# The gates' 16 columns of w_in ride with the first head's v group, which moves to second place, and the scans get a third stream

## The chip, the core and the metric

The kernel runs on one core of one Trainium2 chip. The metric is the device time of one execution in microseconds (us); the kernel before takes 2905.36 us, the median of three runs (2904.51 to 2906.1). A core has five engines that run side by side and wait for each other through semaphores: TensorE (PE in the profile, with its weight loads as PEld), VectorE (DVE), ScalarE (ACT), GpSimd (POOL) and SyncE (SP). Each takes its instructions in the order in which they were built. Transfers between the main memory and the core's own memory are issued from the queues of SP, POOL and ACT; TensorE's results land in eight PSUM banks, of which four are named mm and four sd here.

## The reference, cut to what matters

```python
hn = rmsnorm(x, norm1_w[l])
proj = hn @ w_in[l]                      # 512 x 2048 times 2048 x 11280
conv_out = centred_depthwise_conv(proj[..., :SHORT_CONV_CH], conv_w[l], conv_b[l])
rest = proj[..., SHORT_CONV_CH:]
...                                      # four hyena blocks: long convolutions of conv_out
qk = jax.nn.silu(conv_out[..., 3 * HW:])
v = rest[..., :MW].reshape(B, L, H, dh)
o = jax.nn.sigmoid(rest[..., MW:2 * MW])
g = rest[..., 2 * MW:2 * MW + N_MLSTM_GATES].reshape(B, L, 4, H) + mlstm_gate_bias[l]
h_fwd = mlstm_direction(q, k, v, g[:, :, 0], g[:, :, 1])
h_bwd = flip(mlstm_direction(flip(q), flip(k), flip(v), flip(g[:, :, 2]), flip(g[:, :, 3])))
y_b = o * (h_fwd + h_bwd)
mixed = gate_a * (y_a @ w_branch_a[l]) + gate_b * (y_b @ w_branch_b[l])
x = x + mixed @ w_out[l]
x = x + (jax.nn.silu(gu[..., :FFN_HIDDEN]) * gu[..., FFN_HIDDEN:]) @ w_down[l]   # gu = rmsnorm(x) @ w_gate_up
return rmsnorm(x, norm_f_w)
```

One matrix, w_in, feeds everything: the hyena channels, q, k, v and o of four heads, 16 gate columns, and the two merge gates. The gates g are an input and a forget value of every token, head and direction, 16 numbers a token.

## The kernel before, in words

A product is made in three matmuls (mm3, L72), since every operand is split into a high and a low part: high x high, high x low, low x high. The weights are split by ScalarE (a cast, L170) and VectorE (a subtraction, L171), in units of 256 rows by 256 columns.

The first stage works through the columns of w_in in groups of 256. `group_feat` (L198) holds the weights still and moves 512 tokens, so one of its matmuls has 512 columns; `group_v` (L229) holds the tokens still and moves 256 columns of weights, because v is wanted with the tokens on the partitions. `group_v` needs four PSUM banks of the mm pool, `group_feat` two. The order of the groups is a list written out by hand (`groups`, L1134): the first hyena block, the second, head 0, the third and fourth hyena blocks, heads 1 to 3, the four o groups. `Weights` (L174) makes the split weights two units ahead of their use, in just that order. `w_in_cols` (L1139) yields once after every unit.

`gate_cols` (L431) makes the 16 gate columns behind the first group: it loads 16 columns at a time (rows of 64 bytes), puts their high and low parts side by side into an otherwise zero 128 x 128 tile, and multiplies that with 512 tokens, 32 matmuls in all. The result has the gates on the partitions; four small matmuls with a selection matrix (`sel32`) turn it round, add high and low, and give `gates` with tokens on the partitions.

Beside the groups run the side streams: `stream_b` makes the hyena filters and their spectra and later some sums of x for the merge (`combos_x`), `stream_a` the gate rows (`gate_rows`, L459: logarithms, running sums and running maxima of the gates), then the hyena convolutions and the scan of the heads (`mlstm`, L839), in the order hyena 0 and 1, head 0, hyena 2 and 3, heads 1, 2, 3. `turns` (L971) takes from the streams by turns; every piece states its cost. `drive` (L254) goes through the groups, and gives the side streams 2.6 units of cost per step (RATIO, L1130), saved up to two steps. A stream whose input isn't ready yields "wait". What is left of the streams when the groups are done is run off by a loop behind `drive`. After that a scheduler, which belongs to the framework, orders each engine's instructions by readiness; nothing can pass an instruction that its tile depends on.

A scan of one head loads q and k, splits them, makes four score tiles S (24 matmuls of 512 columns), loads v, and then runs eight units, four in each direction: exponential (ScalarE, L896), mask (GpSimd, L899), product with S (VectorE, L901), split (ScalarE L904, VectorE L905), 3 to 12 matmuls of 258 columns, denominator and result (L927 to L934). Then 8 transposes (L940), two copies (L942) and two stores into d_yb (L943). Its tiles come from the pool pr.

The second stage is the merge: 16 groups of w_in by the class `Winograd`, seven products of 24 matmuls each (L70 with 256 columns), with weights loaded in four quarters (wr and r, L1056). The quarters wr have a pool of their own, the quarters r lie in memory that belonged to pr: their loads wait until the tiles that lay there are done with. Then follow the two branches, w_out, the gate and up matrices and the down matrix, which the change does not touch.

Of the kernel before, what the change touches and what calls it, by code (L numbers as in the profile page):

```python
# [8 lines left out]
F32 = mybir.dt.float32  # L9
# [25 lines left out]
def hybrid_block_kernel(ctx, tc, x, norm1_w, w_in, conv_w, conv_b, filt_w1, filt_b1, filt_freq1,  # L35
# [27 lines left out]
    def mm_ps():  # L63
        return new(pm, "mm")

    def sd_ps():
        return new(psd, "sd")
# [14 lines left out]
        return h, l  # L82


    csm = new(cp, "csm", (P, 3 * P + 16))
# [4 lines left out]
    sel32 = csm[0:32, 3 * P:3 * P + 16]  # L90
    onesf = new(cp, "onesf", (P, P))
    nc.vector.memset(onesf, 1.0)

# [63 lines left out]
        return bc  # L157


    def load_a(w, r0, c0, nk=4, ncol=256):  # L160
        n_tile[0] += 1
        raw = wpool[0].tile([P, nk, ncol], F32, tag="wr", name=f"wr_{n_tile[0]}", bufs=3)
        nc.sync.dma_start(raw, w[r0:r0 + nk * P, c0:c0 + ncol].rearrange("(k p) c -> p k c", p=P))
        return raw

    def split_w(src, shape):
# [7 lines left out]
    class Weights:  # L174
# [6 lines left out]
        def get(self, c0, kb):  # L181
            assert self.units[self.given] == (c0, kb)
            while len(self.made) < min(self.given + 1 + self.ahead, len(self.units)):
                uc, uk = self.units[len(self.made)]
                if uk % 4 == 0:
                    self.raw = load_a(w_in, uk * P, uc)
                self.made.append(split_w(self.raw[:, uk % 4:uk % 4 + 2, :], [P, 2, 256]))
            self.given += 1
            return self.made[self.given - 1]

# [37 lines left out]

    def group_v(w, c0, act, ahead=None):  # L229

        ps = [mm_ps() for _ in range(4)]
        units = w_units(w, 0, KB, c0)
        first = None
        for u in range(0, KB, 2):
            h, l = next(units) if ahead is None else ahead.get(c0, u)
            if u == 0:
                first = (h, l)

            for tb, v, (wh, wl) in ([(tb, u, (h, l)) for tb in (0, 1)] + ([(2, 0, first), (3, 0, first)] if u == 2 else [])
                                    + ([(2, u, (h, l)), (3, u, (h, l))] if u else [])):  # L240
                ts = slice(tb * P, (tb + 1) * P)
                for k in range(2):
                    kb = v + k
                    aH, aL = act[kb]
                    mm3(ps[tb][:, 0:256], aH[:, ts], aL[:, ts], wh[:, k, :], wl[:, k, :],
                        kb == 0, kb == KB - 1)
            yield None
        yield ps
# [177 lines left out]
    a_col = new(cp, "a_col", (P, 2, 4, 4))  # L426
    em_col = new(cp, "em_col", (P, 2, 4, 4))

    gates_t = []

    def gate_cols():  # L431
        gps = mm_ps()
        for u in range(0, KB, 4):
            raw = load_a(w_in, u * P, C_G, 4, 16)
            n_tile[0] += 1
            g = wp.tile([P, 4, P], F32R, tag="wh", name=f"wg_{n_tile[0]}", bufs=4)
            nc.vector.memset(g.bitcast(F32), 0.0)
            nc.vector.tensor_copy(g[:, :, 0:16], raw)
            nc.vector.tensor_tensor(g[:, :, 16:32], raw, g[:, :, 0:16].bitcast(F32), ALU.subtract)
            for k in range(4):  # L440
                kb = u + k
# [3 lines left out]
        gb = new(cp, "gb", (32, 1))  # L445
        nc.vector.memset(gb, 0.0)
        nc.gpsimd.dma_start(gb[0:16], mlstm_gate_bias[0].rearrange("g h -> (g h)").rearrange("(n o) -> n o", o=1))
        gT = gt()
        nc.vector.tensor_tensor(gT[0:32], gps[0:32], rbc[0:32], ALU.mult)
        nc.vector.tensor_scalar(gT[0:32], gT[0:32], gb, None, ALU.add)  # L450
        ps = sd_ps()
        for tb in range(4):
            mm(ps[:, tb * 16:(tb + 1) * 16], gT[0:32, tb * P:(tb + 1) * P], sel32, True, True)
        gates = new(cp, "gates", (P, 4, 2, 2, 4))
        gates_t.append(gates)
        nc.vector.tensor_copy(gates.rearrange("p a b c d -> p (a b c d)"), ps[:, 0:64])
        done.add("gates matmul")

    def gate_rows():  # L459
        yield from need("gates matmul")  # L460
        gates = gates_t[0]

        n = [0]

        def sm(shape=(P, 32)):
            n[0] += 1
            return pr.tile(list(shape), F32, tag=f"gs{n[0]}", name=f"gs{n[0]}", bufs=1)
# [79 lines left out]
    def filter_net():  # L547
        tables = []
        for m in range(4):
            t = gt()  # L550
            nc.sync.dma_start(t, c_dft[m])
            tables.append(t)
        vec = new(ph, "fvec", (P, 4))
        for j, src in enumerate((filt_b1, filt_freq1, filt_b2, filt_freq2)):
            for half in range(2):
                nc.sync.dma_start(vec[half * 64:half * 64 + 64, j:j + 1], src[0].rearrange("(n o) -> n o", o=1))
        w1 = new(ph, "fw1", (33, 2, 64))
        w2 = new(ph, "fw2", (64, 2, 64))
# [5 lines left out]
        nc.sync.dma_start(csm[:, P:3 * P + 16], c_small[:, P:3 * P + 16])  # L564
# [24 lines left out]
        ps = sd_ps()  # L589
        mm(ps, w2.rearrange("p a b -> p (a b)"), h1[0:64], True, True)  # L590
        yield 4
        hh = sin_layer(ps, vec[:, 2:3], vec[:, 3:4])
        h2["H"] = new(ph, "h2H", dt=F32R)
        h2["L"] = new(ph, "h2L", dt=F32R)
        nc.scalar.copy(h2["H"], hh)
        nc.vector.tensor_tensor(h2["L"], hh, h2["H"].bitcast(F32), ALU.subtract)
        yield 4
# [530 lines left out]
    N_PLAIN = 4  # L1128
    AHEAD = 2
    RATIO = 2.6  # L1130
    side = turns(stream_b(), stream_a())

    parts = (("hy", 1), ("hd", 0), ("hy", 2), ("hy", 3), ("hd", 1), ("hd", 2), ("hd", 3))
    groups = [HW, 2 * HW]  # L1134
    for kind, n in parts:
        groups += [b + 256 * n for b in ((0, HW, 2 * HW) if kind == "hy" else (C_Q, C_K, C_V))]
# [405 lines left out]
```

## Time and profile before

| what | value |
|---|---|
| median of three runs | 2905.36 us (2904.51 to 2906.1) |
| the profiled execution's own time | 2905.68 us |
| its span, first to last instruction | 2903.9 us |
| TensorE busy | 2869.5 us (99%) |
| VectorE busy | 2106.6 us (73%) |
| ScalarE busy | 1274.0 us (44%) |
| granted TensorE clock, mean | 0.996 |
| w_in groups end, merge begins | about 834 us |

In a timeline's row stand the start, the duration, the engine, the line, the operation, what it writes and reads, the shape, and how many equal ones follow each other; in brackets the idle time of that engine before it and what ended it. A matmul's duration reaches until its result has landed, and the next starts earlier: the rate is read from the distance between starts. "L70" is the helper mm, so nearly all matmuls have that line, and they are told apart by tiles: mm<-a,wh is a group of w_in, mm<-wh,a a v group, sd<-g,g a scan.

### The profile page before, as it was taken

The page shows a single profiled execution, that of the slowest core. Times are in us where ns is not written, and L with a number is a line of the kernel's source. Part 1 is how long each engine was busy: PE and PEld are TensorE (multiplying, and loading weights), DVE is VectorE, ACT ScalarE, POOL GpSimd, SP SyncE. Part 2 cuts the span into 40 slices and gives each one's busy share as a digit, 9 for nine tenths or more (in the row PEclk, how much of TensorE's full clock was granted, in tenths as well). Part 3 has the DMA queues.
Part 4 walks back from the last instruction along what each step waited for, and adds up shares of the span by engine and source line. Part 5 has one row for each costly group of instructions (what it writes and reads, how often), then busy time and mean ns, then how long its engine had stood idle before and what let it go on. Part 6 is the DMA issues. An engine that isn't in the chain of part 4 may idle for free.

```text
span 2903.9 us, 48189 instructions
## 1 busy us (share of the span) xinstructions
PE 2869.5 (99%) x18412; PEld 2595.7 (89%) x18412; DVE 2106.6 (73%) x3844; ACT 1274.0 (44%) x2267; POOL 186.2 (6%) x431
## 2 busy tenths in 40 slices
PE   9999999999999999999999999999999999999998
PEld 7888887898889999888899999999999998888886
DVE  7897977889478888454549888888888885233336
ACT  5434354436565555222435444444444444233224
POOL 0101011102210001000110000000000000000000
PEclk9999999999999999999999999999999999999999
DMA  5334334334444444743434333333433327343433
GB/s 179 120 109 131 116 120 135 110 115 139 149 126 129 131 140 138 246 138 94 151 122 130 124 118 117 121 119 117 126 123 113 120 89 227 100 124 119 127 109 131
DMA packets 285589, 377.01 MB, mean 130 GB/s; under 512 B 18620, under 2 KB 222852, under 8 KB 285357
## 3 DMA queue, kind: packets, MB, share of 16 engines
q1 hardware_dynamic: 261339, 298.36, 33.2%
q0 software_dynamic: 22752, 73.44, 7.5%
q8 instruction: 144, 2.36, 0.3%
q10 hardware_dynamic: 1266, 2.13, 0.2%
q14 instruction: 88, 0.72, 0.1%
HBM read 326.67 MB, written 47.20 MB: 129 GB/s over the span
## 4 chain that ended last, share of the span: by engine, by line
PE 93%; DVE 3%; DMA 2%; issue 2%; ACT 1%; POOL 0%; SPq 0%; DVEq 0%; POOLq 0%; ACTq 0%
PE mm L70 66%; PE sd L70 26%; DMA wr<-in_w_down_dram 1%; DVE wl L171 0%; DVE st L374 0%; PE sd L289 0%; PE sd L725 0%; PE sd L1301 0%; DMA bt<-d_o 0%; DVE st L371 0%; DVE h L81 0%; DMA xt<-in_x_dram 0%; DMA g<-d_q 0%; DMA g<-d_hy 0%; DVE T L1329 0%
## 5 line engine op out<-in xcount | busy, mean ns | idle before, releaser
L171 DVE TENSOR_TENSOR wl<-wr,wh 128x512 fp32r<-128x512 f32 x512 | 350.6, 688 | 485.9 <-ACT wh L170 480.9
L170 ACT CAST wh<-wr 128x512 fp32r<-128x512 f32 x512 | 316.4, 621 | 763.5 <-PE mm L70 707.7
L70 PE MATMUL mm<-a,wh 128*128 128x512 f32 (+1 forms) x2136 | 626.9, 376 | 0.0
L70 PE MATMUL mm<-T,h 128*128 128x256 f32 x2592 | 463.8, 282 | 3.9 <-ACT h L1047 3.9
L70 PE MATMUL sd<-T,h 128*128 128x256 f32 x2592 | 461.5, 281 | 0.0
L70 PEld LDWEIGHTS mm<-a,wh 128*128 128x128 f32 x2136 | 387.7, 190 | 69.4 <-issue 4.1
L70 PE MATMUL mm<-a,wl 128*128 128x512 f32 (+1 forms) x1068 | 400.8, 375 | 1.9 <-DVE wl L171 1.4
L70 PEld LDWEIGHTS mm<-T,h 128*128 128x128 f32 x2592 | 398.5, 189 | 4.4 <-ACT h L1047 4.4
L70 PE MATMUL mm<-wh,h 128*128 128x512 f32 x1280 | 395.8, 391 | 3.6 <-ACT h L80 3.6
L70 PEld LDWEIGHTS sd<-T,h 128*128 128x128 f32 x2592 | 397.2, 189 | 0.0
L1047 ACT CAST h<-s 128x512 fp32r<-128x512 f32 x395 | 245.0, 621 | 276.6 <-PE sd L70 134.3
L70 PE MATMUL mm<-T,l 128*128 128x256 f32 x1296 | 363.5, 281 | 0.8 <-DVE l L1048 0.8
L70 PE MATMUL sd<-T,l 128*128 128x256 f32 x1296 | 362.7, 280 | 0.0
L70 PEld LDWEIGHTS mm<-wh,h 128*128 128x128 f32 x1280 | 241.4, 189 | 54.0 <-ACT h L80 3.8
L1048 DVE TENSOR_TENSOR l<-s,h 128x512 fp32r<-128x512 f32 x395 | 270.2, 685 | 12.0 <-ACT h L1047 9.6
L1047 ACT CAST h<-r 128x512 fp32r<-128x512 f32 x285 | 177.0, 621 | 215.0 <-PE mm L70 105.3
L70 PE MATMUL mm<-wh,a 128*128 128x256 f32 (+1 forms) x1152 | 259.8, 319 | 0.0
L70 PE MATMUL mm<-wl,h 128*128 128x512 f32 x640 | 249.7, 391 | 0.0
L70 PEld LDWEIGHTS mm<-T,l 128*128 128x128 f32 x1296 | 246.2, 190 | 1.2 <-DVE l L1048 1.2
L70 PEld LDWEIGHTS sd<-T,l 128*128 128x128 f32 x1296 | 245.6, 189 | 0.0
L70 PEld LDWEIGHTS mm<-a,wl 128*128 128x128 f32 x1068 | 202.5, 190 | 37.9 <-DVE wl L171 2.9
L1048 DVE TENSOR_TENSOR l<-r,h 128x512 fp32r<-128x512 f32 x285 | 191.5, 686 | 45.7 <-ACT h L1047 45.5
(365 smaller groups left out, 4358.3 us busy)
## 6 DMA issues: line engine op xcount, KB each, us to landing
r<-in_w_gate_up_dram SPq DMA_DIRECT2D x176, 512.0 KB, 4.7
wr<-in_w_in_dram SPq DMA_DIRECT2D x144, 512.0 KB, 3.8
wr<-in_w_down_dram SPq DMA_DIRECT2D x88, 512.0 KB, 3.6
r<-in_w_in_dram SPq DMA_DIRECT2D x32, 512.0 KB, 4.8
wr<-in_w_out_dram SPq DMA_DIRECT2D x32, 512.0 KB, 4.8
d_h<-xo POOLq DMA_DIRECT2D x44, 256.0 KB, 2.6
hl<-d_h SPq DMA_DIRECT2D x44, 256.0 KB, 3.5
d_g<-xo POOLq DMA_DIRECT2D x32, 256.0 KB, 4.3
```

The source lines that it names most:

```text
L70: nc.tensor.matmul(o, a, b, start=start, stop=stop)
L170: nc.scalar.copy(h, src)
L171: nc.vector.tensor_tensor(l, src, h.bitcast(F32), ALU.subtract)
L1047: nc.scalar.copy(h, a)
L1048: nc.vector.tensor_tensor(l, a, h.bitcast(F32), ALU.subtract)
```

## The change

The gate columns lose their own matmuls. The loads of the first head's v columns bring the 16 gate columns with them, in a second transfer for each load, the split runs over 272 columns, and `group_v` moves 272 columns where it moved 256. The result has the tokens on the partitions at once: four VectorE instructions scale it and add the bias. The first head's v group now stands second in the list of groups, where `gate_cols` stood, and no longer behind q and k of head 0. `gate_rows` becomes a third stream beside the two, and takes its small tiles from one g tile.

```diff
-    def load_a(w, r0, c0, nk=4, ncol=256):
+    def load_a(w, r0, c0, nk=4, ncol=256, extra=False):
...
+        if extra:
+            nc.sync.dma_start(raw[:, :, ncol:n], w[r0:r0 + nk * P, C_G:C_G + 16].rearrange("(k p) c -> p k c", p=P))
...
-                    self.raw = load_a(w_in, uk * P, uc)
-                self.made.append(split_w(self.raw[:, uk % 4:uk % 4 + 2, :], [P, 2, 256]))
+                    self.raw = load_a(w_in, uk * P, uc, extra=uc == C_V)
+                self.made.append(split_w(self.raw[:, uk % 4:uk % 4 + 2, :], [P, 2, 272 if uc == C_V else 256]))
...
-                    mm3(ps[tb][:, 0:256], aH[:, ts], aL[:, ts], wh[:, k, :], wl[:, k, :],
+                    mm3(ps[tb][:, 0:n], aH[:, ts], aL[:, ts], wh[:, k, :], wl[:, k, :],
...
+        if h:
+            yield from v_cols(h)
+
+    def v_cols(h):
         for r in group_v(w_in, C_V + h * 256, X, ahead):
...
+            if h == 0:
+                nc.vector.scalar_tensor_tensor(gates[:, tb].rearrange("p b c d -> p (b c d)"), r[tb][:, 256:272],
+                                               rstd[:, tb:tb + 1], gbias, ALU.mult, ALU.add)
         done.add(("v", h))
+        if h == 0:
+            done.add("gates matmul")
...
-    def gate_cols():
-        gps = mm_ps()
-        for u in range(0, KB, 4):
-            raw = load_a(w_in, u * P, C_G, 4, 16)
...
-                mm(gps, g[:, k, :], X[kb][0], kb == 0, False)
-                mm(gps, g[:, k, :], X[kb][1], False, kb == KB - 1)
-            yield
...
-            mm(ps[:, tb * 16:(tb + 1) * 16], gT[0:32, tb * P:(tb + 1) * P], sel32, True, True)
...
     def stream_a():
-        yield from gate_rows()
         yield from need("filter")
...
-    side = turns(stream_b(), stream_a())
+    side = turns(stream_b(), stream_a(), gate_rows())
...
-    groups = [HW, 2 * HW]
+    groups = [C_V, HW, 2 * HW]
...
-        yield from hyena_cols(0, gate_cols())
+        yield from hyena_cols(0, v_cols(0))
```

In the changed program lines stand some 11 lower in number from `gate_rows` on (L940 is L929, L1056 is L1044).

The first place is TensorE's order behind the first group. mm_233 is that group's second bank, rb are the tiles that spread the norm over a row; before, wg are the gates' weights:

```order
L70 MATMUL mm_233<-a_460,wl_465 128x512
L111 MATMUL sd_481<-csm_72,rows_a_79 128x120
L70 MATMUL sd_538<-csm_72,rb_539 128x128
L70 MATMUL mm_570<-a_214,wg_573 128x512
L70 MATMUL mm_570<-a_215,wg_573 128x512
L70 MATMUL mm_570<-a_218,wg_573 128x512
L70 MATMUL sd_538<-csm_72,rb_542 128x128
L70 MATMUL mm_570<-a_219,wg_573 128x512
```

And now, with wh and wl the first v unit:

```order
L70 MATMUL mm_233<-a_460,wl_465 128x512
L110 MATMUL sd_481<-csm_72,rows_a_79 128x120
L70 MATMUL sd_538<-csm_72,rb_539 128x128
L70 MATMUL mm_573<-wh_580,a_214 128x272
L70 MATMUL mm_573<-wl_581,a_214 128x272
L70 MATMUL mm_573<-wh_580,a_215 128x272
L70 MATMUL mm_573<-wh_580,a_218 128x272
L70 MATMUL sd_538<-csm_72,rb_542 128x128
```

The v group stands where the gates' matmuls stood, with 272 columns.

The second place is TensorE's order at the end of the w_in groups. mm_8768 is the last bank of the last o group, sd<-g are transposes of head 3's scan, and mm_9101 is the first product of the merge. Before:

```order
L70 MATMUL mm_8768<-a_456,wl_8960 128x512
L940 MATMUL sd_8899<-csm_72,g_8645 128x128 x2
L940 MATMUL sd_8899<-csm_72,g_8646 128x128 x2
L940 MATMUL sd_8907<-csm_72,g_8645 128x128 x2
L940 MATMUL sd_8907<-csm_72,g_8646 128x128 x2
L70 MATMUL mm_8768<-a_460,wh_8959 128x512
L70 MATMUL mm_8768<-a_461,wh_8959 128x512
L70 MATMUL mm_8768<-a_460,wl_8960 128x512
L70 MATMUL mm_9101<-a_214,wh_9093 128x256
```

Now, first the end of the last o group and of the first merge product (mm_9033, 24 matmuls), then the start of head 3's scores, then the end of its units, its transposes and the second merge product (mm_9035):

```order
L70 MATMUL mm_8320<-a_460,wl_8630 128x512
L70 MATMUL mm_9033<-a_214,wh_9025 128x256
...
L70 MATMUL mm_9033<-a_456,wl_9030 128x256
L70 MATMUL sd_8723<-g_8667,g_8675 128x512
...
L70 MATMUL sd_8750<-g_8671,g_8680 128x512
L70 MATMUL sd_8797<-g_8765,g_8783 128x258
...
L70 MATMUL sd_8935<-g_8765,g_8917 128x258
L929 MATMUL sd_8953<-csm_72,g_8777 128x128 x2
L929 MATMUL sd_8953<-csm_72,g_8778 128x128 x2
L929 MATMUL sd_8961<-csm_72,g_8777 128x128 x2
L929 MATMUL sd_8961<-csm_72,g_8778 128x128 x2
L70 MATMUL mm_9035<-a_218,h_9065 128x256
```

Head 3's whole scan, 24 score matmuls and 60 of 258 columns, moved from among the last o groups to a place between the first and the second product of the merge.

The third place is SP's queue there, with the semaphores that a load waits for. r_9089 and r_9091 (before), r_9021 and r_9023 (now) are the r quarters of the first merge group. Before:

```order
L1056 DMA wr_9356<-in_w_in_dram 128x4x256 [waits DMAHW6_49,DVE_49,Activation_49]
L1056 DMA r_9089<-in_w_in_dram 128x4x256 [waits DMASW4_49,DMASW5_49,DVE_49,DMASW6_49,PE_49,Pool_49]
L1056 DMA r_9091<-in_w_in_dram 128x4x256 [waits DMASW1_49,DMASW5_49,Activation_49,Pool_49]
L1056 DMA r_9360<-in_w_in_dram 128x4x256 [waits DMASW3_49,DMASW7_49,PE_49,Pool_49]
L1056 DMA r_9362<-in_w_in_dram 128x4x256
```

And now:

```order
L1044 DMA wr_9288<-in_w_in_dram 128x4x256 [waits DMAHW6_49,DVE_49]
L1044 DMA r_9021<-in_w_in_dram 128x4x256 [waits DMASW3_49,DMASW2_49,DMASW5_49,DMASW0_49,DMASW6_49,DVE_49,DMASW7_49,Activation_49,Pool_49]
L1044 DMA r_9023<-in_w_in_dram 128x4x256 [waits DMASW3_49,DMASW1_49,DMASW4_49,DMASW0_49,DMASW5_49,PE_49,Pool_49]
L1044 DMA r_9292<-in_w_in_dram 128x4x256 [waits DMASW4_49,DMASW5_49,DMASW1_49,PE_49]
L1044 DMA r_9294<-in_w_in_dram 128x4x256 [waits DMASW6_49]
```

The pool pr became smaller by the tiles of `gate_rows`, so the r quarters lie over other tiles of it. In the program before, the second r load waits for head 3's last store into d_yb (through DMASW1), the first does not; now the first r load waits for it (through DMASW2), and the others stand behind it in the queue.

More of the change, by code (lines that the diff above doesn't have):

```diff
@@ L82, in split @@
         return h, l
-    csm = new(cp, "csm", (P, 3 * P + 16))
+    csm = new(cp, "csm", (P, 3 * P))
     nc.sync.dma_start(csm[:, 0:P], c_small[:, 0:P])
@@ L89, in hybrid_block_kernel @@
     tril = csm[:, 2 * P:3 * P]
-    sel32 = csm[0:32, 3 * P:3 * P + 16]
     onesf = new(cp, "onesf", (P, P))
@@ L157, in row_broadcast @@
         return bc
-    def load_a(w, r0, c0, nk=4, ncol=256):
+    def load_a(w, r0, c0, nk=4, ncol=256, extra=False):
         n_tile[0] += 1
-        raw = wpool[0].tile([P, nk, ncol], F32, tag="wr", name=f"wr_{n_tile[0]}", bufs=3)
-        nc.sync.dma_start(raw, w[r0:r0 + nk * P, c0:c0 + ncol].rearrange("(k p) c -> p k c", p=P))
+        n = ncol + 16 if extra else ncol
+        raw = wpool[0].tile([P, nk, n], F32, tag="wr", name=f"wr_{n_tile[0]}", bufs=3)
+        nc.sync.dma_start(raw[:, :, 0:ncol], w[r0:r0 + nk * P, c0:c0 + ncol].rearrange("(k p) c -> p k c", p=P))
+        if extra:
+            nc.sync.dma_start(raw[:, :, ncol:n], w[r0:r0 + nk * P, C_G:C_G + 16].rearrange("(k p) c -> p k c", p=P))
         return raw
@@ L231, in group_v @@
         ps = [mm_ps() for _ in range(4)]
+        n = 272 if ahead is not None and c0 == C_V else 256
         units = w_units(w, 0, KB, c0)
@@ L427, in hybrid_block_kernel @@
     em_col = new(cp, "em_col", (P, 2, 4, 4))
-    gates_t = []
-    def gate_cols():
-        gps = mm_ps()
-        for u in range(0, KB, 4):
-            raw = load_a(w_in, u * P, C_G, 4, 16)
[L435 to L441, printed above, removed]
-                mm(gps, g[:, k, :], X[kb][0], kb == 0, False)
-                mm(gps, g[:, k, :], X[kb][1], False, kb == KB - 1)
-            yield
[L445 to L452, printed above, removed]
-            mm(ps[:, tb * 16:(tb + 1) * 16], gT[0:32, tb * P:(tb + 1) * P], sel32, True, True)
[L454 to L457, printed above, removed]
+    gates = new(cp, "gates", (P, 4, 2, 2, 4))
+    gbias = new(cp, "gbias", (P, 16))
+    nc.gpsimd.dma_start(gbias, mlstm_gate_bias[0].rearrange("g h -> (g h)").rearrange("(o n) -> o n", o=1)
+                        .to_broadcast([P, 16]))
     def gate_rows():
         yield from need("gates matmul")
-        gates = gates_t[0]
         n = [0]
+        room = gt()
         def sm(shape=(P, 32)):
-            n[0] += 1
-            return pr.tile(list(shape), F32, tag=f"gs{n[0]}", name=f"gs{n[0]}", bufs=1)
+            n[0] += shape[1]
+            return room[:, n[0] - shape[1]:n[0]]
         f = sm()
@@ L563, in filter_net @@
         nc.sync.dma_start(zt[0:33], c_zt)
-        nc.sync.dma_start(csm[:, P:3 * P + 16], c_small[:, P:3 * P + 16])
+        nc.sync.dma_start(csm[:, P:3 * P], c_small[:, P:3 * P])
         yield "pause"
@@ L1130, in hybrid_block_kernel @@
     RATIO = 2.6
-    side = turns(stream_b(), stream_a())
+    side = turns(stream_b(), stream_a(), gate_rows())
     parts = (("hy", 1), ("hd", 0), ("hy", 2), ("hy", 3), ("hd", 1), ("hd", 2), ("hd", 3))
-    groups = [HW, 2 * HW]
+    groups = [C_V, HW, 2 * HW]
     for kind, n in parts:
-        groups += [b + 256 * n for b in ((0, HW, 2 * HW) if kind == "hy" else (C_Q, C_K, C_V))]
+        groups += [b + 256 * n for b in ((0, HW, 2 * HW) if kind == "hy" else (C_Q, C_K, C_V) if n else (C_Q, C_K))]
     ahead = Weights(groups + [C_O + 256 * g for g in range(4 - N_PLAIN, 4)], AHEAD)
     def w_in_cols():
-        yield from hyena_cols(0, gate_cols())
+        yield from hyena_cols(0, v_cols(0))
         for part in parts:
```

## The prediction

> **What bounds the kernel now.** I read the page first, then TensorE's waits, then the timeline at the three places that the change touches: the gate matmuls at 38 to 53 us, the first v group at 248 us, and the passage from the w_in groups to the merge at 804 to 853 us.
>
> ```profile
> span 2903.9 us, 48189 instructions
> PE 2869.5 (99%) x18412; PEld 2595.7 (89%) x18412; DVE 2106.6 (73%) x3844; ACT 1274.0 (44%) x2267; POOL 186.2 (6%) x431
> PE 93%; DVE 3%; DMA 2%; issue 2%; ACT 1%; POOL 0%; SPq 0%; DVEq 0%; POOLq 0%; ACTq 0%
> ```
>
> TensorE is busy for 99% of the span and makes up 93% of the chain that ended last. So a matmul taken away counts in full where nothing else is late, and so does any idle TensorE time that is added. Its longest wait is this one:
>
> ```profile
> PE mm L70 <- ACT h L1047: 7.1, 3, 3.2
> ```
>
> The wait of 3.2 us lies in the passage to the merge, which is where the change will be decided.
>
> **The gate matmuls (removed).** Before, 32 matmuls of 512 columns and four small ones of 16 columns, with the DVE work between them, stand behind the first group.
>
> ```profile
> 41.58 3.92 PE L70 MATMUL mm<-a,wg 128*128 128x512 f32 x16
> 45.34 0.62 PE L70 MATMUL mm<-a,wh 128*128 128x512 f32 x2
> 46.25 2.02 PE L70 MATMUL mm<-a,wg 128*128 128x512 f32 x8
> 48.20 1.12 PE L70 MATMUL sd<-g,fw 33*128 33x512 f32 x2
> 51.19 0.39 PE L70 MATMUL mm<-a,wh 128*128 128x512 f32 x1
> 51.80 1.03 PE L70 MATMUL sd<-csm,g 32*128 32x16 f32 x8 [0.22 <-DVE g L450]
> 52.77 0.50 PE L70 MATMUL mm<-a,wh 128*128 128x512 f32 x1
> ```
>
> Sixteen take 45.34 - 41.58 = 3.76 us and eight take 1.95 us, 0.235 to 0.244 us each; 32 at 0.235 are 7.5 us. The small ones: a 512-column matmul starts at 51.19 and the next at 52.77; less its own slot (0.227, below) that is 1.35 us. Removed: 8.85 us, all on TensorE's path. The gates' DVE work (memsets, casts) goes too; DVE waits there, so it counts nothing.
>
> **The 16 columns (added).** The v group keeps its 192 matmuls (16 row blocks, 4 token blocks, 3 products) and each gets 272 columns. No 272-column matmul is in the trace; the nearest are 256 and 512.
>
> ```profile
> 249.26 0.40 PE L70 MATMUL mm<-wh,a 128*128 128x256 f32 x2
> 249.62 0.40 PE L70 MATMUL mm<-wh,a 128*128 128x256 f32 x2
> 801.58 0.62 PE L70 MATMUL mm<-a,wh 128*128 128x512 f32 x2
> 802.26 0.62 PE L70 MATMUL mm<-a,wh 128*128 128x512 f32 x2
> ```
>
> Three matmuls of 256 columns repeat every 0.36 us (0.12 each), three of 512 every 0.68 (0.227 each): 0.42 ns a column, so 16 columns are 6.7 ns and 192 of them 1.3 us. Bounds: 0 if something other than columns sets the 0.12, and 192 x 0.107 = 20 us if 272 cost as much as 512. I take 1.3, since 272 is next to 256. The Trainium skill, page "TensorE: Matmul & The Clock Gate", section "Back-to-back issue gap", gives about 131 ns as the sustained spacing at 512 columns; by it the 32 gate matmuls would be worth 4.2 us and not 7.5. The trace's 0.227 disagrees with it, and the sum goes by the trace.
>
> The v group needs four PSUM banks, two of which the first group still holds until its results are multiplied out.
>
> ```profile
> 43.07 1.28 DVE L365 TENSOR_TENSOR pp<-mm,rbc 128x512 f32<-128x512 f32 x2
> ```
>
> The first bank is free near 43.7. TensorE gets there after 31 v matmuls and the rb products, from 38.8 on about 4.7 us, at 43.5. I put 0.3 us on that (0 to 1). The loads of the group take the places in SP's queue that the gate loads had. Its matmuls come earlier and not more often, so moving it costs TensorE nothing itself. Sum so far: -8.85 + 1.3 + 0.3 = -7.3 us.
>
> **What the move does to the scans.** The driver gives the side streams 2.6 units per step. Four gate steps are gone, and 4 x 2.6 = 10.4 units with them; the first hyena channels also come four steps later, since v's eight steps stand where the gates' four stood. Before, the last head's scan ends ahead of the last w_in matmuls. In the built program of the changed kernel it does not: the order in the section on the change shows the whole of head 3's scan (24 score matmuls, 60 of 258 columns, 8 transposes) behind the last w_in group, with only the first merge product (24 matmuls of 256 columns) ahead of it, and the second product behind it. TensorE takes instructions in order, so it waits through that head's chain on ScalarE, GpSimd and VectorE.
>
> ```profile
> 719.43 0.71 ACT L896 ACTIVATE g<-g,a_col 128x512 f32<-128x512 f32 x1
> 720.26 0.30 POOL L899 TENSOR_SCALAR_AFFINE_SELECT g<-g 128x128 f32<-128x128 f32 x1 [3.18 <-issue]
> 720.59 0.69 DVE L901 TENSOR_TENSOR g<-g,g 128x512 f32<-128x512 f32 x1 [1.57 <-POOL g L899]
> 721.31 0.62 ACT L904 CAST g<-g 128x512 fp32r<-128x512 f32 x1 [0.38 <-DVE g L901]
> ...
> 726.41 0.40 ACT L896 ACTIVATE g<-g,a_col 128x128 f32<-128x128 f32 x1
> 727.75 0.30 ACT L904 CAST g<-g 128x128 fp32r<-128x128 f32 x1 [0.88 <-DVE g L901]
> ```
>
> One unit of a scan runs exponential, mask, product, cast: 721.93 - 719.43 = 2.50 us for 512 columns, 728.05 - 726.41 = 1.64 for 128. ScalarE's order has the next unit's exponential behind this unit's cast, so the eight units (512, 384, 256, 128 columns, each twice) follow each other: 8 x 2.07 = 16.5 us at least. Upper bound: the same stretch of head 3 before, spread among w_in matmuls, from its first mask to its transposes.
>
> ```profile
> 806.57 0.29 POOL L899 TENSOR_SCALAR_AFFINE_SELECT g<-g 128x128 f32<-128x128 f32 x1 [1.76 <-ACT g L896]
> 832.40 1.03 PE L940 MATMUL sd<-csm,g 128*128 128x128 f32 x8
> ```
>
> That is 25.8 us. I take 21, the middle: every unit also has its denominator and result between two casts on ScalarE.
>
> Ahead of the units, counted from E, the end of the last w_in matmul, ScalarE's order has a table load, two sigmoids, four splits, and after the scores four evacuations, two casts of v and a table load again.
>
> ```profile
> 803.32 0.64 ACT L422 ACTIVATE st<-st 128x512 f32<-128x512 f32 x1
> 804.48 1.28 ACT L896 ACT_TABLE_LOAD   x1
> ```
>
> ```profile
> L862 ACT ACTIVATE g<-sd x16: 593/598/601, 402.2 to 799.9; 128x512 f32<-128x512 f32 x16
> ```
>
> ```profile
> L170 ACT CAST wh<-wr 128x512 fp32r<-128x512 f32 x512 | 316.4, 621 | 763.5 <-PE mm L70 707.7
> ```
>
> The scores can start after the third split: 1.28 + 2 x 0.64 + 3 x 0.62 = E + 4.4 (TensorE is in the merge product until E + 2.9, so it waits 1.5 us there). 24 scores at 0.227 last to E + 9.8; the last evacuation (0.60), two casts (1.24) and the table load (1.28) end at E + 12.9; the units at E + 33.9. Then comes the way from the scan's transposes to the merge, which before takes this:
>
> ```profile
> 829.70 0.37 SPq L1056 DMA_DIRECT2D r<-in_w_in_dram  x1
> ...
> 833.22 1.06 ACT L942 COPY g<-sd 128x512 f32<-128x512 f32 x2
> 834.16 1.07 POOL L943 DMA_DIRECT2D d_yb<-g  x2
> 837.92 0.37 SPq L1056 DMA_DIRECT2D r<-in_w_in_dram  x1
> 841.65 0.62 ACT L1047 CAST wh<-r 128x512 fp32r<-128x512 f32 x1 [1.53 <-DMA r<-in_w_in_dram]
> ```
>
> From the transposes (832.40) two copies, two stores, their landing, a load of w_in that waits for it, and its cast: the cast starts 9.25 us later. Before, it is the second r load that waits so; the first had gone at 829.7. In the changed program the first r load waits for the last store, and three more stand behind it in SP's queue, so the second product starts at E + 33.9 + 9.25 + 0.62 = E + 43.8. TensorE's own work in that time is 24 x 0.12 + 24 x 0.227 + 60 x 0.12 + 1.0 for the transposes = 16.5 us. Idle: 27.3 us (22.8 with units of 16.5, 32.1 with 25.8).
>
> This takes the place of the wait at the same spot before:
>
> ```profile
> 836.72 0.28 PE L70 MATMUL mm<-a,wl 128*128 128x256 f32 x1
> 840.17 0.50 PE L70 MATMUL mm<-a,h 128*128 128x256 f32 x2 [3.18 <-ACT h L1047]
> ...
> 843.98 0.63 PE L70 MATMUL mm<-a,wh 128*128 128x256 f32 x2
> 844.62 0.63 PE L70 MATMUL mm<-a,wh 128*128 128x256 f32 x2
> ...
> 852.99 0.40 PE L70 MATMUL mm<-T,h 128*128 128x256 f32 x2
> ```
>
> Before, TensorE idles 3.2 us there; the next 72 matmuls take 852.99 - 840.17 = 12.8 us where 72 x 0.12 = 8.6 would do, since three of them take 0.64 us at 844 and not 0.36: a slow clock after the pause, and short waits. I expect about the same 4.2 us behind the longer pause, so it cancels; 1.5 us either way for the range.
>
> **The sum.** Against the profiled execution's own 2905.68 us (its span of 2903.9 and 1.8 around it): -7.3 + 27.3 - 3.2 = +16.8, so 2922.5. The median of the runs is 0.3 below that execution: 2922.2, given as 2922. With units at their bounds: 2917.7 to 2927.0; with 1.5 us for the clock and 3 us for waits in the w_in phase that the new order may add or remove, 2913 to 2932. What a measurement of this kernel can tell from no change is about 0.2%, 5.8 us: 2899.6 to 2911.2.
>
> **Rivals.** First, faster: the end of head 3's scan is hidden as before. Then the 7.3 us count alone: 2898. It decides by the idle time between the first and second merge product: only if that stays under 3.2 + 7.3 = 10.5 us is the kernel not slower. For it speaks that TensorE is 99% busy elsewhere; against it that nothing stands between those products but the scan, and that store, landing and load alone are 9 us. 0.03.
>
> Second, a short tail: the stores, the landing and the load of the first r tile take 6 us and not 9.25 on an empty DMA, the units run at 16.5 us, and the splits and loads of head 3 are under way before E (another 4 us). Idle 16 us: 2911, about the edge of no change, and I count the case as such. 0.07.
>
> Third, a longer tail: the clock drops in the sparse stretch and the scan itself runs slow. At 0.64 for three instead of 0.36, the last matmuls of each unit hold back the next cast, units go to 25.8 us, and the scores become 24 x 0.187 = 4.5 us longer (by the same ratio, 1.78): +16.8 + 4.8 + 4.5, 2932. For it: the trace's clock does fall after 3.2 us of pause. Against it: before the scores the pause is 1.5 us. 0.15. The Trainium skill, page "TensorE: Matmul & The Clock Gate", section "HAM oscillation — how this bites in real kernels", has the rule: a pause longer than a window of about 3.4 us halves the clock, and each later burst starts slow. The trace agrees as far as it goes (0.64 for 0.36 after a pause of 3.18 us, a little under the figure); by the rule the units would all run slow, which is this rival.
>
> The forecast keeps 0.75. The range 2911 to 2932 leaves out the first rival and part of the second and third. Slower by over 0.2%: 0.90; within 0.2%: 0.07; faster: 0.03.
>
> **What would show it.** No gate matmuls at 38 to 50 us and the v group there at about 0.38 us for three matmuls; near 0.46 or more would make the added columns dearer. The w_in groups should end earlier by some 20 us (7.3, and the 13.6 us of head 3 that moved behind them). Then a stretch of about 44 us with TensorE busy for some 16, ScalarE and VectorE in turns, exponentials starting 13 us into it, and an r load that starts only when the last d_yb store has landed. A stretch under 30 us, or merge products inside it, would make the prediction wrong, and so would a new wait of over 3 us ahead of E.

## The result and the profile after

The changed kernel takes 2946.32 us, the median of four runs (2943.87 to 2947.99), against 2905.43 for the kernel before in the same measurement (2904.51 to 2906.1). The ratio is 1.014, with a 95% interval of 1.0125 to 1.0155: slower, by 41 us. The prediction had the sign and a size of 17 us, and its range ended at 2932.

The page of the profiled execution (2944.92 us) and TensorE's longest waits:

```profile
span 2943.2 us, 48100 instructions
PE 2889.2 (98%) x18372; PEld 2607.3 (89%) x18372; DVE 2110.9 (72%) x3832; ACT 1269.6 (43%) x2263; POOL 186.3 (6%) x431
...
PE mm L70 <- ACT h L1035: 11.3, 3, 8.1
PE sd L70 <- ACT g L893: 11.2, 7, 5.5
PE sd L70 <- ACT g L349: 3.4, 3, 2.5
```

The first was 7.1 us before, the second is new in this list, and the third was 1.0 us (there as L345); the longest piece of each (8.1, 5.5 and 2.5 us) lies in the passage to the merge. But TensorE's busy time also rose, by 19.7 us, and that with 40 rows less (32 gate matmuls, and the four small ones, which the profile counts as eight). Where that time went is seen from three places of the trace: the start of the last w_in matmul, the first product with T (the second half of the first merge group), and the last product with T, which ends the gate and up stage. First the kernel before (timeline, and the rows of tile T, with the first and last start):

```profile
833.73 0.39 PE L70 MATMUL mm<-a,wl 128*128 128x512 f32 x1
...
L70 PE MATMUL mm<-T,h x2592: 276/281/415, 853.0 to 2386.6; 128*128 128x256 f32 x200
L70 PE MATMUL sd<-T,h x2592: 277/281/285, 874.4 to 2406.5; 128*128 128x256 f32 x200
```

The same places after:

```profile
822.02 0.40 PE L70 MATMUL mm<-a,wl 128*128 128x512 f32 x1
...
L70 PE MATMUL mm<-T,h x2592: 278/283/582, 878.3 to 2426.1; 128*128 128x256 f32 x200
L70 PE MATMUL sd<-T,h x2592: 278/283/287, 899.7 to 2446.3; 128*128 128x256 f32 x200
```

The w_in groups end 11.7 us earlier (833.7 to 822.0; 20.9 were predicted). The passage from there to the first product with T takes 56.3 us instead of 19.3, so 37.0 more. From that product to the end of gate and up it is 1568.0 us instead of 1553.5: 14.5 more, in stages that the diff does not touch. The rest of the span is 0.5 shorter. -11.7 + 37.0 + 14.5 - 0.5 = 39.3, the difference of the spans.

The passage after, in TensorE's timeline; the first row is the last of the first merge product's, then come head 3's scores, its units, its transposes and the second merge product:

```profile
824.98 0.28 PE L70 MATMUL mm<-a,wl 128*128 128x256 f32 x1
827.80 5.83 PE L70 MATMUL sd<-g,g 128*128 128x512 f32 x24 [2.54 <-ACT g L349]
839.17 5.47 PE L70 MATMUL sd<-g,g 128*128 128x258 f32 x27 [5.54 <-ACT g L893]
...
857.23 1.97 PE L929 MATMUL sd<-csm,g 128*128 128x128 f32 x8 [1.30 <-DVE g L923]
867.30 0.79 PE L70 MATMUL mm<-a,h 128*128 128x256 f32 x2 [8.11 <-ACT h L1035]
```

And on ScalarE and in the queues of POOL and SP: the first exponential, the last of the two stores, the four r loads, and the cast that the second product waits for:

```profile
836.65 0.72 ACT L885 ACTIVATE g<-g,a_col 128x512 f32<-128x512 f32 x1
...
860.12 0.55 POOL L932 DMA_DIRECT2D d_yb<-g  x1 [0.29 <-ACT g L931]
...
862.70 2.25 SPq L1044 DMA_DIRECT2D r<-in_w_in_dram  x4
...
866.63 0.62 ACT L1035 CAST h<-r 128x512 fp32r<-128x512 f32 x1 [6.81 <-DMA r<-in_w_in_dram]
```

That is the chain of the prediction, step by step, with E at 822.25 (the last w_in matmul's start and its slot of 0.23): the scores start at E + 5.6 (predicted 4.4), the exponentials at E + 14.4 (12.9), from there to the transposes it is 20.6 us (21), from the transposes to the second product 10.1 (9.9), and the second product starts at E + 45.05 (43.8).

The other loss is in the matmuls themselves. Gate and up alone, the same 2464 of its matmuls, in the kernel before and then in the changed one:

```profile
L70 PE MATMUL sd<-T,h x2464: 277/282/285, 1551.9 to 2406.5; 128*128 128x256 f32 x190
```

```profile
L70 PE MATMUL sd<-T,h x2464: 280/283/287, 1579.6 to 2446.3; 128*128 128x256 f32 x190
```

854.6 us became 866.7, 12.1 more, with no wait in it. With the other three kinds of that stage (mm<-T,h 2464, and 1232 each with l) there are 7392 matmuls, so each takes 1.6 ns more. And in the w_in groups, eight times three matmuls of 512 columns without any gap, before and after:

```profile
640.18 0.62 PE L70 MATMUL mm<-a,wh 128*128 128x512 f32 x2
...
645.64 0.61 PE L70 MATMUL mm<-a,wh 128*128 128x512 f32 x2
```

```profile
639.62 0.62 PE L70 MATMUL mm<-a,wh 128*128 128x512 f32 x2
...
645.17 0.62 PE L70 MATMUL mm<-a,wh 128*128 128x512 f32 x2
```

5.46 us became 5.55: 227.5 ns each became 231.3.

**Two theories of the slower matmuls.** Theory A: the places of the operands. The change gives tiles of the first pools other sizes: the first pool becomes 32 bytes smaller in all, and the split weights and loads of w_in get slots of 2176 and 4352 bytes instead of 2048 and 4096. In the built program before, w_in's split weights and activations all lie at 256 modulo 512 bytes; now the activations lie at 480 and the weights at 96, 224, 352 or 480. The gate and up weights go from 256 to 224, while three quarters of the activations there (42 tiles of 56) stay at 480. Theory B: the changed order of work on the other engines and the transfers slows them. The passage at the end of w_in is a separate cause, and has experiments of its own.

### The profile page after: what moved, and what is told of

Same layout as the page of the kernel before. It is cut to its first block, busy times and chain, and to the rows that moved or that the text cites. A ratio compares the mean times of both kernels' runs of the same rounds, so it can differ in the third digit from the quotient of the medians.

```text
span 2943.2 us, 48100 instructions
## 1 busy us (share of the span) xinstructions
PE 2889.2 (98%) x18372; PEld 2607.3 (89%) x18372; DVE 2110.9 (72%) x3832; ACT 1269.6 (43%) x2263; POOL 186.3 (6%) x431
## 4 chain that ended last, share of the span: by engine, by line
PE 69%; DVE 1%; DMA 1%; issue 1%; ACT 0%; POOL 0%; SPq 0%; POOLq 0%; DVEq 0%; ACTq 0%
PE mm L70 48%; PE sd L70 21%; DMA wr<-in_w_down_dram 1%; PE sd L1289 0%; DVE s L1052 0%; DVE h L81 0%; DMA r<-in_w_in_dram 0%; DVE T L1317 0%; DVE l L1036 0%; ACT h L80 0%; DMA d_yb<-g 0%; PE sd L929 0%; DVE x L1429 0%; DVE g L890 0%; DVE x L1428 0%
## 5 line engine op out<-in xcount | busy, mean ns | idle before, releaser
L173 DVE TENSOR_TENSOR wl<-wr,wh 128x512 fp32r<-128x512 f32 (+1 forms) x512 | 352.2, 692 | 487.7 <-ACT wh L172 483.9
L172 ACT CAST wh<-wr 128x512 fp32r<-128x512 f32 (+1 forms) x512 | 316.1, 621 | 767.4 <-PE mm L70 714.0
L70 PE MATMUL mm<-T,h 128*128 128x256 f32 x2592 | 471.0, 284 | 3.2 <-ACT h L1035 3.2
L70 PE MATMUL sd<-T,h 128*128 128x256 f32 x2592 | 468.0, 283 | 0.0
L70 PE MATMUL mm<-wh,a 128*128 128x256 f32 (+2 forms) x1152 | 263.2, 321 | 0.9 <-DVE pp L369 0.9
```

The lines of the kernel that those rows point to most:

```text
L70: nc.tensor.matmul(o, a, b, start=start, stop=stop)
L172: nc.scalar.copy(h, src)
L173: nc.vector.tensor_tensor(l, src, h.bitcast(F32), ALU.subtract)
```

## The experiments

In all of them "before" is the kernel before on the same chip.

**lower_32: theory A in gate and up.** The bias tile of 4 bytes (32 with its slot) moves into the unused end of another tile:

```diff
-    ssq_c = new(cp, "ssq_c", (P, 4, 5))
+    ssq_g = new(cp, "ssq_c", (P, 21))
+    ssq_c = ssq_g[:, 0:20].rearrange("p (a b) -> p a b", a=4)
...
-        gb = new(cp, "gb", (32, 1))
+        gb = ssq_g[0:32, 20:21]
```

> The kernel before, all instructions in the same order on TensorE, ScalarE and SyncE; one 4-byte tile less in the first pool, so that all tiles above it lie 32 bytes lower. Theory A (where the two operands of a matmul lie sets its rate): the w_in groups keep the distance between their operands, so their 512-column matmuls stay at 0.227 us; in the gate and up stage the split weights move by 32 bytes and most activations stay, as in the changed kernel, so its 256-column matmuls go from 118 to 120 ns and the stage gets 11.7 us longer: 2917 us. Theory B (the changed order of work, or other engines' traffic, slows the matmuls): nothing is changed in either, 2905 us.

Measured: 2917.67 us, ratio 1.0041 (1.0026 to 1.0056). Gate and up in its trace:

```profile
L70 PE MATMUL sd<-T,h x2464: 283/283/283, 1553.0 to 2419.7; 128*128 128x256 f32 x190
```

866.7 us, the stage's time in the changed kernel to the tenth. The w_in groups end at 835.0, 1.2 later than before. So 32 bytes, with the same instructions in the same order, cost 12 us; theory B is out for this stage. But the row says more: all 2464 matmuls became alike (283 from lowest to highest), also the quarter of them whose activations moved down together with the weights and kept the distance 0. By the distances between starts that quarter went from 118.9 to 120.0 ns, and the other three quarters from 118.2 to 120.0. The places set the rate, then, but the distance alone does not.

**apart_128: theory A in the w_in groups.** An unused tile between the weights and the activations:

```diff
     next(first_group)
+    wp.tile([P, 32], F32, tag="gap", name="gap")
     conv_columns()
```

> The kernel before with every instruction in the same order; an unused tile of 128 bytes between the split weights and the activations of the first stage. Theory A: operands of the w_in groups that lay at the same place modulo 512 bytes are now 128 apart; at that distance the changed kernel's 512-column matmuls take 232.6 ns and not 227.2, which for 24 groups of 96 is 12.4 us, and some 2 us in the branches: 2918 to 2920 us, with the gate and up stage unchanged. Theory B: 2905 us.

Measured: 2914.39 us, ratio 1.0031 (1.002 to 1.0043). The same eight times three matmuls, the end of w_in, and gate and up:

```profile
640.19 0.62 PE L70 MATMUL mm<-a,wh 128*128 128x512 f32 x2
...
645.76 0.62 PE L70 MATMUL mm<-a,wh 128*128 128x512 f32 x2
...
841.88 0.39 PE L70 MATMUL mm<-a,wl 128*128 128x512 f32 x1
...
L70 PE MATMUL sd<-T,h x2464: 277/282/285, 1561.3 to 2415.9; 128*128 128x256 f32 x190
```

5.57 us, 232.1 ns each; w_in ends 8.2 us later than before; gate and up takes 854.6, as before. The place is right, the total smaller than expected: 8.2 us over the 2304 matmuls of the 24 groups are 3.5 ns each, where I had put 5.4 on all of them, the difference of the two distances that I had compared in the trace. The rows above differ by 4.6 ns a matmul, so the rate changed by more than the end of w_in shows. A part went to the v groups: their 768 matmuls of 256 columns got the same new distance and became faster, from 119.8 to 118.7 ns by the distances between starts in the two traces, 0.9 us in all. Where the rest went was not traced.

**after_aligned: theory A undone in the changed kernel.** The first pool gets its 32 bytes back, the loads get slots of a multiple of 512 bytes, and the 272-column weights go into one tile for each row block, half of them in the slots of 2048 bytes and half in another pool:

```diff
-    csm = new(cp, "csm", (P, 3 * P))
+    csm = new(cp, "csm", (P, 3 * P + 8))
...
-        raw = wpool[0].tile([P, nk, n], F32, tag="wr", name=f"wr_{n_tile[0]}", bufs=3)
+        raw = wpool[0].tile([P, nk, n + 16 if extra else n], F32, tag="wr", name=f"wr_{n_tile[0]}", bufs=3)
...
+            pool, th, tl = (wp, "wh", "wl") if k == 0 else (ph, "xh", "xl")
+            h.append(pool.tile([P, 272], F32R, tag=th, name=f"vh_{n_tile[0]}", bufs=4))
+            l.append(pool.tile([P, 272], F32R, tag=tl, name=f"vl_{n_tile[0]}", bufs=4))
```

> The changed kernel with the operands of all stages at the same distances as before (weight tiles 2048 bytes apart again, the first pool 32 bytes larger); the 272-column weights of the first v group are split row block by row block, which adds 8 casts and 8 subtractions. Theory A: the w_in groups win some 8 us, the branches 2, the gate and up stage 11.7 back: 2925 us, near what was predicted for the scans' tail alone. Theory B: 2946 us or a little more.

Measured: 2923.81 us (2922.07 to 2926.79), ratio to before 1.0063 (1.0048 to 1.0078).

```profile
815.89 0.39 PE L70 MATMUL mm<-a,wl 128*128 128x512 f32 x1
...
821.69 5.83 PE L70 MATMUL sd<-g,g 128*128 128x512 f32 x24 [2.54 <-ACT g L362]
...
L70 PE MATMUL sd<-T,h x2464: 277/282/285, 1569.5 to 2424.1; 128*128 128x256 f32 x190
```

Gate and up is back at 854.6, w_in ends 6.1 us earlier than in the changed kernel, and the scan still lies in the passage, with the same first wait (2.54). Of the 41 us, 22.5 were the places of the operands (23.1 if each kernel is taken against before in its own measurement). What is left, 17.8 us over before, is near the prediction's 16.8.

**after_ratio_2_7: the tail undone in the changed kernel.**

```diff
-    RATIO = 2.6
+    RATIO = 2.7
```

> The changed kernel with 2.7 in place of 2.6 units of side work per step, so that head 3's scan is built ahead of the last w_in matmul again. If the scan's chain behind the last w_in matmul costs what the trace shows (45.0 us until the second merge product, 16.5 of it TensorE's work, against a wait of 3.2 before): 2946.3 - 25.3 = 2921 us. If the wait only moves to another place (the r loads, which wait for the last store of the scan in either order): 2935 to 2946 us.

Measured: 2928.56 us, ratio to before 1.0078 (1.0063 to 1.0093). The tail's cost is real, 17.8 us of the 25.3 come back. The other 7.5 are lost ahead of it: the passage goes from 56.3 to 19.5 us (843.3 to 862.8 in this trace), but w_in ends at 843.3, 21.3 later than in the changed kernel, where head 3's own work on TensorE is 13.6.

**before_tail: the tail alone, in the kernel before.**

```diff
-    RATIO = 2.6
+    RATIO = 2.46
```

> The kernel before with 2.46 in place of 2.6 units of side work per step and nothing else: head 3's scan (24 score matmuls, 60 of 258 columns, 8 transposes) is built behind the last w_in matmul, as in the changed kernel, with the gate matmuls and the tiles' places of before. If the scan's tail alone costs what the changed kernel's trace shows at that place (56.3 us from the last w_in matmul to the first matmul of the second half of the first merge group, against 19.2 before, less the 13.6 us of TensorE's work that leave the w_in groups): +23.5, 2929 us. If the waiting load there matters (the first r load waits for the scan's last store in the changed kernel, only the second here): up to 8 us less, 2921 us.

Measured: 2927.36 us, ratio 1.0073 (1.0058 to 1.0088): +22.1 us. The lower rate alone, with the gate matmuls and the layout of before, gives the passage:

```profile
816.88 0.39 PE L70 MATMUL mm<-a,wl 128*128 128x512 f32 x1
...
856.89 0.80 PE L70 MATMUL mm<-a,h 128*128 128x256 f32 x2 [1.19 <-ACT h L1047]
863.40 0.51 PE L70 MATMUL mm<-a,wh 128*128 128x256 f32 x2 [3.29 <-ACT wh L1047]
...
L70 PE MATMUL mm<-T,h x2592: 276/281/583, 874.4 to 2407.3; 128*128 128x256 f32 x200
```

57.5 us from the last w_in matmul to the first product with T. The first r load does not wait for the scan's last store here, so the second product starts earlier in the passage; then it waits for the next load instead, and the sum is the same. Which of the r loads waits for the store makes no difference worth a microsecond.

**aligned_ratio_2_7: both causes undone.** The edits of after_aligned and after_ratio_2_7 together.

> The changed kernel with both causes undone: operands at the distances of before, and 2.7 units per step. If they add up: 2923.8 - (2946.3 - 2928.6) = 2906 us. If the 7.5 us by which the higher rate fell short (2928.6 where 2921 was expected) were waits that the layout caused: 2898 us.

Measured: 2908.3 us (2905.4 to 2914.81 in 10 runs), ratio 1.001 (1.000 to 1.0019). The two add up (2906 were expected); the 7.5 us were not the layout's. The kernel without gate matmuls ends no earlier than the one with them. TensorE's waits from 60 to 820 us say where part of it went, first before, then here:

```profile
PE sd L70 <- ACT g L345: 1.0, 1, 1.0
PE mm L70 <- DVE wl L171: 1.0, 1, 1.0
PE sd L725 <- DMA g<-d_hy: 1.0, 1, 1.0
PE sd L70 <- DVE g L678: 0.9, 3, 0.5
PE sd L70 <- DVE g L346: 0.5, 1, 0.5
```

```profile
PE sd L727 <- DMA g<-d_hy: 3.3, 3, 1.9
PE mm L70 <- DVE wl L173: 2.1, 4, 0.5
PE sd L70 <- ACT g L362: 1.8, 2, 1.4
PE mm L70 <- ACT st L432: 1.7, 1, 1.7
PE sd L70 <- DVE g L363: 0.8, 1, 0.8
PE mm L70 <- DVE pp L382: 0.5, 1, 0.5
PE sd L70 <- DVE g L680: 0.4, 1, 0.4
```

4.4 us before, 10.6 here: by the releasers, TensorE waits longer for the hyena inputs' loads, for the weight splits of the groups, for the casts of the scans, and once for an evacuation of a v group. 6.2 of the 7.3 us are given back there.

**aligned_ratio_2_8.** The same with 2.8.

> The changed kernel with operands at the distances of before and 2.8 units per step: head 3's scan ends some 120 matmuls ahead of the last w_in matmul, so its stores have landed when the first r load is due. If that hides the wait of 4.8 us that is left at 2.7: 2903.5 us. If the faster side streams lose as much at their own waits in the w_in groups: 2908 us or more.

Measured: 2910.04 us (2908.46 to 2911.9), ratio 1.0017 (1.0008 to 1.0026). The second case: w_in ends at 841.6, 5.9 later than at 2.7, and the passage wins 3.5 of it (15.9 against 19.4 us).

**raise_480, raise_128, lower_64, raise_64: other distances.** One unused tile in the first pool of the kernel before, of 480, 128, 448 and 64 bytes, for instance:

```diff
+    new(cp, "gap", (P, 120))
     onesf = new(cp, "onesf", (P, P))
```

> The kernel before, every instruction in the same order, an unused tile of 480 bytes in the first pool. If only the place modulo 512 bytes counts, this is the same as 32 bytes lower: 2917.7 us. If the distance itself counts, or a larger modulus: another time, near 2906 or above.

> The kernel before, every instruction in the same order, an unused tile of 128 bytes in the first pool: the w_in operands stay at distance 0, the gate and up weights go from 224 bytes below most of their activations (modulo 512) to 96 below. That distance is in no trace so far; by theory A the gate and up stage changes and the w_in groups don't: between 2899 (1 ns less for each of some 7000 matmuls) and 2918 us.

> The kernel before, every instruction in the same order, an unused tile of 448 bytes in the first pool, the same modulo 512 as 64 bytes lower: w_in operands stay at distance 0, the gate and up weights go from 224 to 288 bytes below most of their activations. Pairs that far apart the other way round are in the trace of the merge before, at 117.1 ns against 118.2. If the distance alone counts, up to 1 ns less for some 5300 matmuls: 2900 us. If 118 at 224 was a special place, as 96 and 256 were slower by 2 ns: 2915 to 2918 us.

> The kernel before, every instruction in the same order, an unused tile of 64 bytes in the first pool: distance 160 in the gate and up stage, which no trace shows yet; 96 and 256 gave 120 ns, 224 gave 118. Between 2905 (as at 224) and 2917 us (as at 96 and 256).

The gate and up row of each, in this order:

```profile
L70 PE MATMUL sd<-T,h x2464: 280/283/287, 1552.4 to 2419.0; 128*128 128x256 f32 x190
```

```profile
L70 PE MATMUL sd<-T,h x2464: 278/282/285, 1552.3 to 2416.9; 128*128 128x256 f32 x190
```

```profile
L70 PE MATMUL sd<-T,h x2464: 278/280/284, 1555.5 to 2410.1; 128*128 128x256 f32 x190
```

```profile
L70 PE MATMUL sd<-T,h x2464: 277/280/283, 1554.6 to 2405.2; 128*128 128x256 f32 x190
```

| kernel | weights below most activations, modulo 512 | gate and up stage | time | ratio (95%) |
|---|---|---|---|---|
| before | 224 | 854.6 us | | |
| lower_32 | 256 | 866.7 | 2917.67 | 1.0041 (1.0026 to 1.0056) |
| raise_480 | 256 | 866.6 | 2917.14 | 1.0038 (1.0023 to 1.0053) |
| raise_128 | 96 | 864.6 | 2916.05 | 1.0037 (1.0023 to 1.0051) |
| lower_64 | 288 | 854.6 | 2901.65 | 0.9992 (0.9981 to 1.0002) |
| raise_64 | 160 | 850.6 | 2904.19 | 0.9997 (0.9987 to 1.0006) |

Here raise_480 does what lower_32 does: one pair of kernels with places 512 bytes apart, and they act alike. lower_64 was expected at 2900 with a faster stage; the stage is as before, and the time can't be told from before's. raise_64 wins 4.0 us in the stage and does not show them in the time: from its first product with T (852.9) to that stage it takes 2.8 us longer than before (701.7 against 698.9), probably since the tile moves the pools of those stages as well.

**gap_64: the better distance alone.** 64 bytes in front of the gate and up pools only, in the kernel before:

```diff
+    gap = ctx.enter_context(tc.tile_pool(name="gap", bufs=1, reuse_waits="tile"))
+    new(gap, "gap", (P, 16))
     t3_cm = tc.tile_pool(name="t3", bufs=14, reuse_waits="tile")
```

> The kernel before, every instruction in the same order, an unused tile of 64 bytes in front of the gate and up stage's pools only. Theory A, with the distance of 160 bytes that took 4.0 us off this stage in raise_64 (854.6 to 850.6 us) and the w_in, merge and branch stages left where they were: 2904.6 - 4.0 = 2900.6 us. Theory B: 2904.6 us.

Measured: 2902.17 us against 2906.18, ratio 0.9986 (0.9977 to 0.9995).

```profile
L70 PE MATMUL sd<-T,h x2464: 277/280/283, 1552.7 to 2403.2; 128*128 128x256 f32 x190
```

850.5 us for the stage, 4.1 less, and 4.0 in the time. It is the one kernel of the study that is faster than both with an interval clear of 1, by a seventh of a per cent.

## Why the prediction was wrong

**The passage: right.** Its terms came out within 1.5 us each, and its end at E + 45.05 for 43.8; after_ratio_2_7 and before_tail show the cause from both sides. The 27.3 us of idle time were the scan's chain, and the chain was on ScalarE and in the stores and loads, as worked out. The granted clock did fall to half in the pause:

```profile
838.00:858.00 20.00, 12.24 (x64) 10.44 (x65) 11.89 (x36) 9.40 (x27) 2.77 (x8) 0.84 0.06 14
858.00:868.00 10.00, 1.89 (x8) 1.29 (x6) 1.35 (x2) 1.79 (x3) 1.11 (x2) 0.50 0.58 185
```

The column behind the five engines is the granted clock: 0.84, then 0.50; the first matmuls behind the pause take 0.64 us for three, up to 870.3. The rule of the Trainium skill, page "TensorE: Matmul & The Clock Gate", section "HAM oscillation — how this bites in real kernels", by which a long pause halves the clock for what follows, agrees with these rows. It did not bring the third rival: the units took 20.6 us, not that rival's 25.8.

**The gate matmuls and the 16 columns: right in themselves.** No wg matmul is left, and the v group runs at 54 matmuls in 6.79 us, 0.377 per three (0.38 predicted):

```profile
43.06 0.41 PE L70 MATMUL mm<-wh,a 128*128 128x272 f32 x2
...
49.85 0.41 PE L70 MATMUL mm<-wh,a 128*128 128x272 f32 x2
```

That is 126 ns each, 1.1 us more for 192 than at 0.12 (1.3 predicted). The PSUM bank wait is 0.9 us (0.3, bounds 0 to 1).

**The step that failed: the sum had no term for matmuls that the change does not touch.** The prediction took 0.227 and 0.12 us from the trace of before for every group, and carried only the clock and "3 us for waits in the w_in phase" as the unknown. But the edits to csm, gb, wr, wh and wl are edits to where tiles lie. lower_32 and apart_128 show, with unchanged instructions, that this sets the rate, and after_aligned gives its price in the changed kernel: 22.5 us, by the traces 12.1 of it in gate and up, 3.3 in the merge and the branches ahead of it, 6.1 in w_in, and the rest in the passage and behind gate and up. The miss in the total is this: without it the forecast of 2922 stands beside 2923.8, and that these two are so close is in part luck.

**Two smaller errors that cancelled.** The tail was worked out at 24.1 us (27.3 less 3.2) and costs 22.1 in before_tail. And the 7.3 us of the gate part were to show in full. At the end of w_in, after_aligned is only 1.0 us ahead of before_tail (815.9 and 816.9), which has the same passage and layout and the gate matmuls; in the whole time it is 3 to 4 us, and at 2.7 units nothing. Part of it went into the waits listed above; why the order of the side work makes them was not tested one by one, and stays open.

**The rivals.** Faster, the short tail and the long tail were all about the passage, and none of them happened. In the third the scores' price has a slip (0.227 times 0.78 is 0.177 and not 0.187, so 4.2 us for 4.5), which changes nothing. The real one was missing: a change of tile sizes that slows the matmuls of another stage.

## What to carry to other kernels

A diff that changes the size of a tile in a long-lived pool moves every tile above it, and here that moved untouched stages by up to 12 us: compare the places of the two operands of the heaviest matmuls before and after, and shift one pool by an unused tile to see what that alone does. When work leaves a paced main loop, count what it paced: here four steps less, and hyena channels that come four steps later (the two were not told apart), put one head's scan behind the loop, at three times what was to be saved (22.1 us in before_tail against 7.3). And before the freed time is booked as gain, ask at which rate the side work must run to be done in time, and which waits come with that rate.

## What the runs showed of the hardware

The rate of these matmuls depends on where the moving operand and the weights lie. In w_in, 512 moving columns, three-matmul rows in full flow: 227.5 ns at distance 0, 232.1 at 128 bytes (8.2 us at the end of w_in in apart_128). When both operands move together these keep their rate: in lower_32, with both 32 bytes lower, the w_in groups end 1.2 us later than before and not 8. In gate and up, 256 columns, with three quarters of the matmuls at the distance named: 850.6 us for the stage at 160 bytes, 854.6 at 224 and 288, 864.6 at 96 and 866.7 at 256, so 1.6 ns a matmul between 224 and 256.

No simple rule over these distances is claimed, and three readings of the traces, by the distances between starts, speak against one. First, the quarter of gate and up that stays at distance 0 takes 120.0 ns in lower_32, where both operands lie at 224 modulo 512, for 118.9 before; so more than their own distance counts, the place itself or the matmuls next in order. For the latter speaks that in the kernel before the merge's matmuls with T and wh, at the same places and at distance 0, take 119.7 ns; no run separates the two. Second, in raise_128 that quarter takes 118.7 ns beside 120.0 for those at distance 96, in the same stage with the same weights, so the distance does count. Third, the sign turns with the number of columns: in apart_128, 128 bytes apart makes the 512 columns slower and the 256 columns of the v groups faster.

Whether 512 bytes is the period is open. The pair of lower_32 and raise_480 agrees with it, but the changed kernel's w_in matmuls take the same 229.5 ns at the distances 0 and 256, and 232.8 to 232.9 at 128 and 384, so that it may be shorter for them. Which part of the chip the two operands meet in was not tried.
